# Gate/up of a hybrid encoder layer: where the part stores are issued, and how the next group's operands are split

## The chip, the cores and the metric

One core of one Trainium2 chip runs the whole kernel. The metric is the device time of one execution in microseconds (us); the median of three runs before the change is 2669.16 us. The engines are named as in the profile: PE (TensorE), PEld (its weight loads), DVE (VectorE), ACT (ScalarE), POOL (GpSimd), and SP (SyncE, which here only issues DMAs). ACT issues DMAs too, from the same in-order queue as its arithmetic.

## The reference

One layer of a streaming encoder is computed for 17 tiles of 128 tokens: 2048 prompt tokens and 8 streams of 16. A mixer (gated delta rule and a short convolution) and an output projection come first. What matters here is the last part, the feed-forward network:

```python
h = rmsnorm(x, norm_ffn_pre)
f = (jax.nn.silu(h @ w_gate) * (h @ w_up)) @ w_down
x = x + rmsnorm(f, norm_ffn_post)
```

with a model width of 1024 and a hidden width of 2816, all in float32.

## The kernel before

**Number format.** Each float32 operand v is split into a high part h, v rounded to the matmul's format by a cast on ACT, and a low part l = v - h, a subtraction on DVE or POOL. A product is three matmuls, hh, hl and lh. For the tokens' operands this split is made in `ffn_prep` (cast L893, subtraction L894), for the weights in `gu_weights` (cast L938, subtraction L939).

**Gate/up.** The tokens form three groups `FGROUPS` of 6, 6 and 5 tiles; the hidden width forms 22 columns f of 128 (`NF`). For each group the kernel walks over all 22 columns; one column of one group is called a block, (group, f). Gate and up are treated together as a 2x2 block product with the Strassen-Winograd scheme, so that a block takes 7 products instead of 8. A product has 12 matmuls (4 slices of the model width, 3 matmuls each, L963), a block 84, each with half a group's tokens as moving data: 384 columns for groups 0 and 1, 320 for group 2.

The 7 token operands of a group are named in `PARTS`: B11, T3, T1, T2, B21, T4, B22. Each consists of 4 slices (k), each a high tile xh and a low tile xl. T3 and a first sum are made by `ffn_sums`, T2 and T4 by one subtraction per slice inside `ffn_prep` (L887, L889), in place on the loaded half-tiles, so that one has to follow the other. The xh and xl tiles exist once: the split for the next group may be written only when PE has read the old group's tile for the last time.

**One block.** `gu_start` makes the first four products (B11, T3, T1, T2) into four PSUM banks b1, b3, b4, b2. `gate_up` then copies b1, b3 and b4 out by ACT (L999, L1000, L1001), and the other three products (B21, T4, B22) are added into those banks; each may begin only after the copy of its bank. Then come the recombination and the gating: u2 (DVE L1007), two additions on POOL (L1008, L1013), a SiLU (ACT L1010), c21 and c12 (DVE L1012, L1014), a second SiLU (ACT L1015), and the two gated results v1, v2 (DVE L1027, L1028). While this runs, `gu_start` of the next block goes ahead into four other banks.

Even and odd columns are combined for the down projection: an even block keeps v1 and v2 in a11 and a21; an odd block writes its own into a tile `pt` with six planes and makes four sums of them (L1034 to L1037). `pt` has one buffer. An odd block then stores `pt` to DRAM (`partd`), one DMA for each pair of token tiles, three in groups 0 and 1 and two in group 2 (L1039); an even block stores a11 with one DMA (L1041). Group 2 also stores its unpaired tile into `lastd` (L1031). All of these are issued on ACT's queue at the end of `gate_up`.

**Weights.** In group 0 the weights of a column are loaded, combined into sA to sD (L929 to L932), split, and the split ones are partly written to DRAM (`fsplit`); groups 1 and 2 reload them, and split again only three of the seven, except for the first two columns (`NSP`), of which all seven are reloaded. `ffetch` in `gate_up` runs one block ahead. The tiles sA to sD are used by group 0 alone.

**Change of group.** During columns 4 to 11 of a group the next group's eight half-tiles h are loaded, at column 16 `ffn_sums` runs on them, and after the last column `ffn_prep` makes all seven operands: 28 casts on ACT, 28 subtractions (L894), for even k on POOL and for odd k on DVE, and the 8 differences L887 and L889 on DVE. For group 0 the same work is done during the output projection.

**What sets the order.** The program is written in this order, but `TileContext(schedule_with_timeline_sim=True)` lets a planner sort the instructions of each engine: it steps through its own estimate of time, and of the instructions whose inputs it deems ready the one written first is issued first. An instruction written later can thus run earlier if it is ready earlier. On the chip each engine keeps the planned order, whatever comes late. Waits for tiles, banks and DMAs are set by the framework.

Of the kernel before, what the change touches and what calls it, by code (L numbers as in the profile page):

```python
# [10 lines left out]
F32R = mybir.dt.float32r  # L11
# [6 lines left out]
P = 128  # L18
# [4 lines left out]
NF = DFF // P  # L23
# [20 lines left out]
FGROUPS = [list(range(0, 6)), list(range(6, 12)), list(range(12, 17))]  # L44
# [25 lines left out]
def kernel(  # L70
# [28 lines left out]
    nc = tc.nc  # L99
    V, A, G, T = nc.vector, nc.scalar, nc.gpsimd, nc.tensor  # L100
# [7 lines left out]
    partd = [[dram.tile([len(g) // 2, P, 7, len(c) // 2, P], F32, name=f"partd{gi}_{ch}") for ch, c in enumerate(FCHUNKS)]  # L108
             for gi, g in enumerate(FGROUPS)]
    lastd = [dram.tile([P, 2, len(c) // 2, P], F32, name=f"lastd{ch}") for ch, c in enumerate(FCHUNKS)]  # L110
# [742 lines left out]
    KH = KD // 2  # L853
    PARTS = ("B11", "T3", "T1", "T2", "B21", "T4", "B22")
    HW = max(len(g) for g in FGROUPS) * P // 2
    with ExitStack() as ph:
        fp = ph.enter_context(tc.tile_pool(name="fp", bufs=1, reuse_waits="tile"))
# [12 lines left out]
        def ffn_sums(gi, hs, fs):  # L870
            hw = len(FGROUPS[gi]) * P // 2
            t3 = []
            for k in range(KH):
                b11, b12, b21, b22 = blocks(gi, hs, k)
                t3.append(fs.tile([P, HW], F32, tag="t3", name="ft3", bufs=KH)[:, :hw])
                V.tensor_sub(t3[k], b22, b12)
                V.tensor_sub(b12, b12, b11)
            return t3

        def ffn_prep(gi, hs, t3):  # L880
            hw = len(FGROUPS[gi]) * P // 2
            X = {nm: ([], []) for nm in PARTS}
            for nm in PARTS:
                for k in range(KH):
                    b11, b12, b21, b22 = blocks(gi, hs, k)
                    if nm == "T2":
                        V.tensor_sub(b12, b22, b12)  # L887
                    elif nm == "T4":
                        V.tensor_sub(b12, b21, b12)  # L889
                    v = {"B11": b11, "B21": b21, "B22": b22, "T3": t3[k]}.get(nm, b12)  # L890
                    h = fp.tile([P, HW], F32R, tag=f"xh{nm}{k}", name="xh")
                    l = fp.tile([P, HW], F32R, tag=f"xl{nm}{k}", name="xl")
                    A.copy(h[:, :hw], v)  # L893
                    (V if k % 2 else G).tensor_tensor(  # L894
                        out=l[:, :hw], in0=v, in1=h[:, :hw].bitcast(F32), op=ALU.subtract)
                    X[nm][0].append(h)
                    X[nm][1].append(l)
            return X

        with tc.tile_pool(name="fs", bufs=1, reuse_waits="tile") as fs:  # L900
            hs = list(ffn_load(0, fs))
            hid = ffn_prep(0, hs, ffn_sums(0, hs, fs))
        fe = ph.enter_context(tc.tile_pool(name="fe", bufs=1, reuse_waits="tile"))

        nw, early, wl = [0], [], []
# [50 lines left out]
        def product(ps, w, b, first):  # L956
            wh, wl = w
            bh, bl = b
            hw = ps.shape[-1]
            for k in range(KH):  # L960
                c = slice(k * P, (k + 1) * P)
                for ci, (w_, b_) in enumerate(((wh, bh), (wh, bl), (wl, bh))):
                    T.matmul(ps, w_[:, c], b_[k][:, :hw], start=(first and k == 0 and ci == 0),  # L963
                             stop=(k == KH - 1 and ci == 2), skip_group_check=not first)

        def gu_start(gi, f, X):
            hw = len(FGROUPS[gi]) * P // 2
# [17 lines left out]
        fd = side.enter_context(tc.tile_pool(name="fd", bufs=1, reuse_waits="tile", side="right"))  # L985
        ffetch(5 - NWE)

        def gate_up(gi, f, X, banks):
            n = len(FGROUPS[gi])
            hw = n * P // 2  # L990
            g_, f_, W, _ = fpend.pop(0)

            def ct(nm):
                return fb.tile([P, HW], F32, tag=nm, name=nm)[:, :hw]

            w = dict(zip(("A12", "A22", "S4"), W[4:]))
            b1, b3, b4, b2 = banks
            s1, s7, s5 = ct("m1"), ct("m7"), ct("m5")
            A.copy(s1, b1)  # L999
            A.copy(s7, b3)  # L1000
            A.copy(s5, b4)  # L1001
            product(b1, w["A12"], X["B21"], False)
            product(b3, w["A22"], X["T4"], False)
            product(b4, w["S4"], X["B22"], False)
            ffetch()
            u2 = ct("u2")
            V.tensor_add(u2, s1, b2)  # L1007
            G.tensor_tensor(out=s7, in0=s7, in1=s5, op=ALU.add)  # L1008
            sg0 = ct("m5")
            A.activation(sg0, b1, AF.Silu)  # L1010
            c21, c12 = ct("c21"), ct("c12")
            V.tensor_add(c21, u2, b3)  # L1012
            G.tensor_tensor(out=s7, in0=s7, in1=u2, op=ALU.add)  # L1013
            V.tensor_add(c12, u2, b4)  # L1014
            A.activation(c12, c12, AF.Silu)  # L1015
            ch, kk = FCH[f]
            q, c = kk // 2, len(FCHUNKS[ch]) // 2
            if kk % 2 == 0:
                a11 = fb.tile([P, HW], F32, tag="a11", name="a11", bufs=2)
                a21 = fb.tile([P, HW], F32, tag="a21", name="a21", bufs=2)  # L1020
                held[gi] = a11, a21
                v1, v2 = a11[:, :hw], a21[:, :hw]
            else:
                a11, a21 = held[gi]
                pt = fb.tile([P, 6, HW], F32, tag="pt", name="pt")
                v1, v2 = pt[:, 3, :hw], pt[:, 4, :hw]
            V.tensor_mul(v1, c21, sg0)  # L1027
            V.tensor_mul(v2, s7, c12)  # L1028
            if n % 2:
                for vi, v in enumerate((v1, v2)):  # L1030
                    nc.scalar.dma_start(out=lastd[ch][:, kk % 2, q, vi * 64:vi * 64 + 64], in_=v[:, hw - 64:hw])  # L1031
            if kk % 2:
                a11, a21, a12, a22 = a11[:, :hw], a21[:, :hw], v1, v2
                V.tensor_add(pt[:, 0, :hw], a21, a22)  # L1034
                V.tensor_sub(pt[:, 1, :hw], a11, a21)
                V.tensor_sub(pt[:, 2, :hw], pt[:, 0, :hw], a11)
                V.tensor_sub(pt[:, 5, :hw], pt[:, 2, :hw], a12)  # L1037
                for j in range(n // 2):
                    nc.scalar.dma_start(out=partd[gi][ch][j, :, 1:7, q, :], in_=pt[:, :, j * P:(j + 1) * P])  # L1039
            else:  # L1040
                nc.scalar.dma_start(out=partd[gi][ch][:, :, 0, q, :].rearrange("j p c -> p j c"),  # L1041
                                    in_=v1[:, :n // 2 * P].rearrange("p (j c) -> p j c", c=P))

        held, first_parts = {}, []
        for gi in range(len(FGROUPS)):
            if gi:
                hid = ffn_prep(gi, hs, t3)
            if gi + 1 < len(FGROUPS):
                hload, hs = ffn_load(gi + 1, fd), []
            for f in range(NF):  # L1050
                gate_up(gi, f, hid, started or gu_start(gi, f, hid))
                started = None
                if gi + 1 < len(FGROUPS):
                    if 4 <= f < 4 + KD:
                        with tc.issue_after(wl[0].ins):
                            hs.append(next(hload))
                    if f == NF - 6:
                        t3 = ffn_sums(gi + 1, hs, fd)
                elif f == 10:
                    side.close()  # L1060
                    dr = late.enter_context(tc.tile_pool(name="dr", bufs=1, reuse_waits="tile", side="right"))
                    c = len(FCHUNKS[0]) // 2
                    a = dr.tile([P, 2, c * P], F32, name="ar0")
                    nc.sync.dma_start(out=a, in_=partd[0][0][0, :, 0:2].rearrange("p i q c -> p i (q c)"))
                    first_parts = [dr.tile([P, 2, c * P], F32R, name=f"as0{i}") for i in range(2)]
                    for i, b in enumerate(first_parts):
                        A.copy(b[:, 0], a[:, i])
                        V.tensor_sub(b[:, 1], a[:, i], b[:, 0].bitcast(F32))
                    dprep += [down_chunk(ch) for ch in dorder]
                    prep_step(2)  # L1070
                elif 10 < f <= 10 + NDR:
                    prep_step(1)
# [203 lines left out]
```

## Time and profile before

| what | value |
|---|---|
| three runs | 2666.46, 2669.16, 2670.29 us |
| profiled execution, first to last instruction (its span) | 2659.7 us |
| the median of the runs less this span | 9.5 us |
| mean granted clock of PE | 0.978 |
| gate/up: first to last matmul of L963 | 1225.0 to 2167 us |
| DVE busy in gate/up (1225 to 2167.5) | 518.9 us |
| ACT, POOL busy there | 323.0, 473.7 us |
| DMA share there | 0.80 |

The span is that of one profiled execution; what lies around it in a run's time, the start and the end of a launch, is not in the profile, which gives no other time of that execution. In the profile's rows a line number is that of the kernel file; `xl<-fh,xh` names the tile written and the tiles read. An idle time in brackets is that of the engine just before the instruction, and the name behind the arrow is what ended it. "ACTq" is ACT's queue issuing a DMA, "issue" is time for which the profile shows no wait. The window view lists, for each stretch, its length, the engine's busy time and the instructions that touch it, the granted clock, the DMA share and the GB/s.

### The profile page before, as it was taken

The page shows a single profiled execution, that of the slowest core. Times are in us where ns is not written, and L with a number is a line of the kernel's source. Part 1 is how long each engine was busy: PE and PEld are TensorE (multiplying, and loading weights), DVE is VectorE, ACT ScalarE, POOL GpSimd, SP SyncE. Part 2 cuts the span into 40 slices and gives each one's busy share as a digit, 9 for nine tenths or more (in the row PEclk, how much of TensorE's full clock was granted, in tenths as well). Part 3 has the DMA queues.
Part 4 walks back from the last instruction along what each step waited for, and adds up shares of the span by engine and source line. Part 5 has one row for each costly group of instructions (what it writes and reads, how often), then busy time and mean ns, then how long its engine had stood idle before and what let it go on. Part 6 is the DMA issues. An engine that isn't in the chain of part 4 may idle for free.

```text
span 2659.7 us, 42363 instructions
## 1 busy us (share of the span) xinstructions
PE 2533.2 (95%) x15129; PEld 2357.1 (89%) x15129; DVE 1717.3 (65%) x3403; ACT 971.8 (37%) x2337; POOL 939.5 (35%) x841
## 2 busy tenths in 40 slices
PE   7989899999999989999999999999899999999997
PEld 6889789989899987878999999999899987887776
DVE  7788567667575875676978863433633344677698
ACT  5535115142251524433434432222323335333343
POOL 2321001000010210224556654443544445555563
PEclk9999989999999998999999999999999999999999
DMA  6876576666657555667877777877888852443365
GB/s 206 293 255 243 166 245 216 226 225 239 214 207 248 177 182 173 230 214 250 309 261 271 265 259 250 282 247 240 286 287 278 276 169 87 129 123 119 126 217 176
DMA packets 322403, 589.46 MB, mean 222 GB/s; under 512 B 57116, under 2 KB 206304, under 8 KB 303376
## 3 DMA queue, kind: packets, MB, share of 16 engines
q1 hardware_dynamic: 193600, 510.01, 56.7%
q10 hardware_dynamic: 128592, 76.74, 9.5%
q8 instruction: 120, 1.97, 0.3%
q14 instruction: 91, 0.75, 0.1%
HBM read 424.60 MB, written 162.05 MB: 221 GB/s over the span
## 4 chain that ended last, share of the span: by engine, by line
PE 67%; DVE 13%; DMA 8%; issue 4%; ACT 3%; POOL 2%; SPq 1%; ACTq 1%; DVEq 0%; POOLq 0%
PE fbank L963 28%; PE dbank L136 16%; PE fbank L1122 10%; PE tbank L758 3%; PE dbank L758 3%; DMA w<-wsplit 2%; DMA wr<-in_w_in 1%; DVE acc L367 1%; DVE xl L894 1%; POOL dw L829 1%; DMA dr<-in_w_dn 1%; DVE xr L1137 1%; DVE acc L1081 1%; DVE acc L1136 1%; DMA xt<-in_x 1%
## 5 line engine op out<-in xcount | busy, mean ns | idle before, releaser
L963 PE MATMUL fbank<-xh,fw 128*128 128x384 f32 (+1 forms) x3696 | 904.2, 327 | 19.7 <-ACT m L999 12.1
L136 PE MATMUL dbank<-hi,w 128*128 128x384 f32 (+1 forms) x2688 | 691.9, 336 | 16.6 <-DMA w<-wsplit 9.7
L963 PEld LDWEIGHTS fbank<-xh,fw 128*128 128x128 f32 x3696 | 654.9, 189 | 23.4 <-ACT m L999 14.2
L963 PE MATMUL fbank<-xl,fw 128*128 128x384 f32 (+1 forms) x1848 | 604.2, 327 | 0.0
L136 PEld LDWEIGHTS dbank<-hi,w 128*128 128x128 f32 x2688 | 484.8, 193 | 22.8 <-POOL w L340 8.4
L1122 PE MATMUL fbank<-dw,as 128*128 128x512 f32 x1980 | 463.2, 395 | 14.3 <-ACT dw L827 5.0
L1122 PEld LDWEIGHTS fbank<-dw,as 128*128 128x128 f32 x1980 | 372.0, 189 | 105.2 <-DVE acc L1081 7.4
L136 PE MATMUL dbank<-lo,w 128*128 128x384 f32 (+1 forms) x1344 | 449.5, 335 | 0.0
L963 PEld LDWEIGHTS fbank<-xl,fw 128*128 128x128 f32 x1848 | 348.9, 189 | 0.0
L136 PEld LDWEIGHTS dbank<-lo,w 128*128 128x128 f32 x1344 | 259.0, 193 | 1.7 <-issue 0.8
L1106 POOL TENSOR_TENSOR as<-ar,as 128x256 fp32r<-128x256 f32 (+1 forms) x207 | 188.2, 918 | 171.8 <-ACT as L1103 170.4
L939 POOL TENSOR_TENSOR fw<-rg,fw 128x512 fp32r<-128x512 f32 x124 | 176.5, 1424 | 180.9 <-ACT fw L938 180.7
L1081 DVE TENSOR_TENSOR acc<-acc,fbank 128x512 f32<-128x512 f32 x248 | 166.6, 682 | 99.6 <-PE fbank L1122 79.6
L1103 ACT CAST as<-ar 128x256 fp32r<-128x256 f32 (+1 forms) x288 | 118.3, 427 | 181.8 <-PE fbank L1122 132.7
L340 POOL TENSOR_TENSOR w<-wr,w 128x512 fp32r<-128x512 f32 x49 | 78.3, 1599 | 223.6 <-ACT w L338 188.0
L938 ACT CAST fw<-rg 128x512 fp32r<-128x512 f32 x124 | 77.5, 625 | 185.1 <-PE fbank L963 147.9
L367 DVE SCALAR_TENSOR_TENSOR acc<-R,cw,acc 128x384 f32<-128x384 f32 (+1 forms) x216 | 131.0, 609 | 2.0
L1007 DVE TENSOR_TENSOR u<-m,fbank 128x384 f32<-128x384 f32 (+1 forms) x66 | 34.8, 528 | 143.3 <-PE fbank L963 130.4
L1008 POOL TENSOR_TENSOR m<-m,m 128x384 f32<-128x384 f32 (+1 forms) x66 | 69.4, 1051 | 159.5 <-ACT m L1001 119.0
L939 POOL TENSOR_TENSOR fw<-ru,fw 128x512 fp32r<-128x512 f32 x62 | 92.3, 1488 | 85.8 <-ACT fw L938 70.2
L1012 DVE TENSOR_TENSOR c<-u,fbank 128x384 f32<-128x384 f32 (+1 forms) x66 | 34.9, 528 | 127.8 <-PE fbank L963 127.6
L552 POOL MEMSET AU<- 32x128 f32 x16 | 3.2, 197 | 281.0 <-PE gbank L538 272.1
(322 smaller groups left out, 3807.2 us busy)
## 6 DMA issues: line engine op xcount, KB each, us to landing
w<-wsplit SPq DMA_DIRECT2D x119, 1024.0 KB, 6.0
fw<-fsplit SPq DMA_DIRECT2D x188, 512.0 KB, 4.7
fsplit<-fw SPq DMA_DIRECT2D x94, 512.0 KB, 4.1
partd<-pt ACTq DMA_DIRECT2D x88, 384.0 KB, 6.0
rg<-in_w_gu SPq DMA_DIRECT2D x62, 512.0 KB, 3.7
wsplit<-w SPq DMA_DIRECT2D x28, 1024.0 KB, 4.7
wr<-in_w_in SPq DMA_DIRECT2D x98, 256.0 KB, 4.4
ar<-partd SPq DMA_DIRECT2D x48, 384.0 KB, 3.3
```

The costliest lines, as they stand in the source:

```text
L136: T.matmul(ps, l, r, start=(i == 0), stop=(i == n - 1))
L340: e.tensor_tensor(out=wl[:, c], in0=wr, in1=wh[:, c].bitcast(F32), op=ALU.subtract)
L367: V.scalar_tensor_tensor(acc, raw(d), w[:, d:d + 1], acc, op0=ALU.mult, op1=ALU.add)
L758: T.matmul(pss[n], m_[:, j, :], w_[k][:, n * 512:(n + 1) * 512], start=(k == 0 and ci == 0), stop=(k == KD - 1 and ci == 2))
L938: A.copy(w[:, 0], v)
L939: e.tensor_tensor(out=w[:, 1], in0=v, in1=w[:, 0].bitcast(F32), op=ALU.subtract)
L963: T.matmul(ps, w_[:, c], b_[k][:, :hw], start=(first and k == 0 and ci == 0), stop=(k == KH - 1 and ci == 2), skip_group_check=not first)
L1008: G.tensor_tensor(out=s7, in0=s7, in1=s5, op=ALU.add)
L1081: V.tensor_add(dst, dst, ps)
L1103: ins = A.copy(a[:, 0, :n], v)
L1106: e.tensor_tensor(out=a[:, 1, :n], in0=v, in1=a[:, 0, :n].bitcast(F32), op=ALU.subtract)
L1122: T.matmul(ps, a[:, x_, q * P:(q + 1) * P], w[:, y_], start=(start and q == 0 and ci == 0), stop=(q == c - 1 and ci == 2), skip_group_chec ...
```

## The change

Two things are done.

The part stores (L1031, L1039, L1041) are no longer issued where they are written: their arguments are put in a list `queued`, and the next block's `gate_up` issues them, in the program's order, right after its three bank copies. The last block of the last group issues its own at once.

The next group's operands are made in steps: `ffn_prep` now takes the dictionary X to fill and the names to make. B11 is made after column 20 of the old group. For group 1 it goes to tiles of its own, the high parts into four new tiles of the pool `fd`, the low parts into sA to sD; for group 2 it goes into the old B11 tiles, which are free since the end of group 0. T3, T1 and T2 are made after the last column, as before. B21, T4 and B22 are made inside the first block of the new group, behind its bank copies and the queued stores. For groups 1 and 2 all subtractions L894 are on DVE; for group 0 DVE and POOL trade even and odd k.

```diff
-        def ffn_prep(gi, hs, t3):
+        def ffn_prep(gi, hs, t3, X, names):
             hw = len(FGROUPS[gi]) * P // 2
-            X = {nm: ([], []) for nm in PARTS}
-            for nm in PARTS:
+            for nm in names:
+                X[nm] = ([], [])
                 for k in range(KH):
...
-                    h = fp.tile([P, HW], F32R, tag=f"xh{nm}{k}", name="xh")
-                    l = fp.tile([P, HW], F32R, tag=f"xl{nm}{k}", name="xl")
+                    if gi == 1 and nm == "B11":
+                        h = fd.tile([P, HW], F32R, tag="xh", name="xh", bufs=KH)
+                        l = fe.tile([P, 512], F32R, tag="s" + "ABCD"[k], name="xl")
+                    else:
+                        h = fp.tile([P, HW], F32R, tag=f"xh{nm}{k}", name="xh")
+                        l = fp.tile([P, HW], F32R, tag=f"xl{nm}{k}", name="xl")
                     A.copy(h[:, :hw], v)
-                    (V if k % 2 else G).tensor_tensor(
+                    (G if not gi and k % 2 else V).tensor_tensor(
                         out=l[:, :hw], in0=v, in1=h[:, :hw].bitcast(F32), op=ALU.subtract)
...
+        FIRST, REST = PARTS[:4], PARTS[4:]
...
-            hid = ffn_prep(0, hs, ffn_sums(0, hs, fs))
+            hid = ffn_prep(0, hs, ffn_sums(0, hs, fs), {}, PARTS)
...
             A.copy(s5, b4)
+            for q in queued:
+                nc.scalar.dma_start(**q)
+            queued.clear()
+            if "B21" not in X:
+                ffn_prep(gi, hold["hs"], hold["t3"], X, REST)
             product(b1, w["A12"], X["B21"], False)
...
-                    nc.scalar.dma_start(out=partd[gi][ch][j, :, 1:7, q, :], in_=pt[:, :, j * P:(j + 1) * P])
+                    queued.append(dict(out=partd[gi][ch][j, :, 1:7, q, :], in_=pt[:, :, j * P:(j + 1) * P]))
...
+            if (gi, f) == (len(FGROUPS) - 1, NF - 1):
+                for q in queued:
+                    nc.scalar.dma_start(**q)
...
             if gi:
-                hid = ffn_prep(gi, hs, t3)
+                hid = ffn_prep(gi, hs, t3, hold["X"], FIRST[1:])
+                hold.update(hs=hs, t3=t3)
...
                     if f == NF - 6:
                         t3 = ffn_sums(gi + 1, hs, fd)
+                    elif f == NF - 2:
+                        hold["X"] = ffn_prep(gi + 1, hs, t3, {}, FIRST[:1])
```

The stores of L1031 and L1041 are queued in the same way.

More of the change, by code (lines that the diff above doesn't have):

```diff
@@ L1030, in gate_up @@
                 for vi, v in enumerate((v1, v2)):
-                    nc.scalar.dma_start(out=lastd[ch][:, kk % 2, q, vi * 64:vi * 64 + 64], in_=v[:, hw - 64:hw])
+                    queued.append(dict(out=lastd[ch][:, kk % 2, q, vi * 64:vi * 64 + 64], in_=v[:, hw - 64:hw]))
             if kk % 2:
@@ L1038, in gate_up @@
                 for j in range(n // 2):
-                    nc.scalar.dma_start(out=partd[gi][ch][j, :, 1:7, q, :], in_=pt[:, :, j * P:(j + 1) * P])
+                    queued.append(dict(out=partd[gi][ch][j, :, 1:7, q, :], in_=pt[:, :, j * P:(j + 1) * P]))
             else:
-                nc.scalar.dma_start(out=partd[gi][ch][:, :, 0, q, :].rearrange("j p c -> p j c"),
-                                    in_=v1[:, :n // 2 * P].rearrange("p (j c) -> p j c", c=P))
-        held, first_parts = {}, []
+                queued.append(dict(out=partd[gi][ch][:, :, 0, q, :].rearrange("j p c -> p j c"),
+                                   in_=v1[:, :n // 2 * P].rearrange("p (j c) -> p j c", c=P)))
+            if (gi, f) == (len(FGROUPS) - 1, NF - 1):
+                for q in queued:
+                    nc.scalar.dma_start(**q)
+        held, first_parts, queued, hold = {}, [], [], {}
         for gi in range(len(FGROUPS)):
             if gi:
-                hid = ffn_prep(gi, hs, t3)
+                hid = ffn_prep(gi, hs, t3, hold["X"], FIRST[1:])
+                hold.update(hs=hs, t3=t3)
             if gi + 1 < len(FGROUPS):
```

## The prediction

> **What bounds the kernel now.** I read the page first: 2659.7 us of span, TensorE (PE) busy for 95% of it. So only stretches where PE is not fed count. The change touches gate/up alone, so I cut that stage by PE's matmuls of L963 in windows at the blocks' first matmuls (a block is one column f of one group: 84 matmuls, 22 blocks to a group). The columns are stretch, length, PE busy (instructions touching it), granted clock, DMA share, GB/s.
>
> ```profile
> span 2659.7 us, 42363 instructions
> PE 2533.2 (95%) x15129; PEld 2357.1 (89%) x15129; DVE 1717.3 (65%) x3403; ACT 971.8 (37%) x2337; POOL 939.5 (35%) x841
> ...
> 1225.04:1247.08 22.04, 16.76 (x84) 0.92 0.56 185
> 1247.08:1400.17 153.09, 147.82 (x842) 1.00 0.86 300
> 1400.17:1560.33 160.16, 160.16 (x926) 1.00 0.79 276
> 1560.33:1581.22 20.89, 17.19 (x85) 0.84 0.61 187
> 1581.22:1886.98 305.76, 305.76 (x1766) 1.00 0.80 259
> 1886.98:1908.37 21.39, 14.19 (x86) 0.93 0.94 315
> 1908.37:2167.00 258.63, 258.63 (x1764) 1.00 0.80 258
> ```
>
> The fifth stretch holds 21 blocks of group 1 with PE never idle: 305.76 / 21 = 14.56 us a block, PE's own pace. The last gives group 2, with narrower tiles, 258.63 / 21 = 12.32. Against these, four stretches lose time: block (0,0) 22.04 - 14.56 = 7.48; blocks (0,1) to (0,10) 153.09 - 145.60 = 7.49; the first block of group 1 20.89 - 14.56 = 6.33; the first of group 2 21.39 - 12.32 = 9.07. Blocks (0,11) to (0,21) are 11 x 14.56 = 160.16 to the last digit. So the stage holds 30.4 us of loss; the change can touch the last three, **22.9 us**. That is the ceiling.
>
> PE's timeline and its waits say what ends each loss; the last row is PE's weight loads waiting for L1001 within 1240 to 1410 us.
>
> ```profile
> 1572.52 0.69 PE L963 MATMUL fbank<-xh,fw 128*128 128x384 f32 x1 [3.70 <-ACT m L999]
> ...
> 1896.52 0.41 PE L963 MATMUL fbank<-xh,fw 128*128 128x320 f32 x1 [2.35 <-ACT m L999]
> 1905.15 0.48 PE L963 MATMUL fbank<-xh,fw 128*128 128x320 f32 x1 [4.85 <-ACT m L1001]
> ...
> PEld fbank L963 <- ACT m L1001: 4.0, 4, 2.0
> ```
>
> Always it is a copy out of a bank by ScalarE (ACT): the second half of a block may not add into a bank before its copy is out. At the start of group 1 the idle 3.70 costs 6.33 because the clock drops (0.84 in that row). Why was the copy late? ACT's timeline, a window of DVE, and the groups of DVE and of POOL from 1548.43 to 1571.0:
>
> ```profile
> 1571.57 0.52 ACT L1015 ACTIVATE c<-c 128x384 f32<-128x384 f32 x1 [1.22 <-DVE c L1014]
> 1572.00 0.46 ACT L999 COPY m<-fbank 128x384 f32<-128x384 f32 x1
> ...
> 1548.43:1572.00 23.57, 23.54 (x27) 0.98 0.79 269
> ...
> L894 DVE TENSOR_TENSOR xl<-fh,xh 128x384 fp32r<-128x384 f32 x10 | 11.9, 1202 | 0.0
> L889 DVE TENSOR_TENSOR fh<-fh 128x384 f32<-128x384 f32 x4 | 4.4, 1118 | 0.0
> L894 DVE TENSOR_TENSOR xl<-ft,xh 128x384 fp32r<-128x384 f32 x2 | 2.7, 1367 | 0.0
> L887 DVE TENSOR_TENSOR fh<-fh 128x384 f32<-128x384 f32 x4 | 2.5, 642 | 0.0
> ...
> L894 POOL TENSOR_TENSOR xl<-fh,xh 128x384 fp32r<-128x384 f32 x11 | 13.6, 1261 | 3.8 <-ACT xh L893 3.8
> ```
>
> L999 stands behind the SiLU L1015, that behind VectorE's (DVE) L1014, and DVE has been busy 23.54 of 23.57 us with the next group's operands: up to L1014 (its 0.5 us end where L1015 starts, so it began near 1571.0), 12 splits (L894) and 8 differences, 21.5 us together, while POOL makes the other splits. The price of one depends on the neighbour, as the timelines of both show:
>
> ```profile
> 1556.29 1.03 DVE L887 TENSOR_TENSOR fh<-fh 128x384 f32<-128x384 f32 x2
> 1557.23 0.55 DVE L894 TENSOR_TENSOR xl<-fh,xh 128x384 fp32r<-128x384 f32 x1
> 1563.35 3.95 DVE L894 TENSOR_TENSOR xl<-fh,xh 128x384 fp32r<-128x384 f32 x3
> ...
> 1554.52 1.32 POOL L1008 TENSOR_TENSOR m<-m,m 128x384 f32<-128x384 f32 x1
> 1557.94 3.77 POOL L894 TENSOR_TENSOR xl<-fh,xh 128x384 fp32r<-128x384 f32 x3 [2.10 <-ACT xh L893]
> 1561.67 1.33 POOL L1013 TENSOR_TENSOR m<-m,u 128x384 f32<-128x384 f32 x1
> 1562.97 3.91 POOL L894 TENSOR_TENSOR xl<-fh,xh 128x384 fp32r<-128x384 f32 x3
> ```
>
> POOL is idle from 1555.84 to 1557.94: there DVE gets through two operations in 0.94 us (1556.29 to the next start, 1557.23), 0.47 each. Beside three POOL splits, three of DVE take 3.95: 1.3 each. That factor is the heart of the sum.
>
> **The change part by part. First, the operands.** Nothing is saved in count: 28 casts, 28 splits and 8 differences per group stay, all 28 splits now on DVE. Four (B11) go ahead of the last block; their room is DVE's idle before this row, after the old spare tiles' last reader:
>
> ```profile
> 1540.04 0.69 DVE L939 TENSOR_TENSOR fw<-sD,fw 128x512 fp32r<-128x512 f32 x1 [3.17 <-ACT fw L938]
> ...
> 1543.88 0.56 DVE L1012 TENSOR_TENSOR c<-u,fbank 128x384 f32<-128x384 f32 x1 [2.69 <-PE fbank L963]
> ```
>
> 4 x 0.47 = 1.9 of 2.69 us: hidden (without that cover, 1.9). POOL keeps its two additions per block (L1008, L1013), each holding one DVE operation at 1.3 instead of 0.47: 1.7 us. Suppose, against the change, that all 24 other splits still come before L1014: from 1548.43, 32 x 0.47 = 15.0, three block operations (L1035, L1007, L1012) x 0.47 = 1.4, plus 1.7, gives 1566.5; L1014 0.5, L1015 0.5, L999 0.5: **1568.0**. PE's second half of that block is due at 1560.33 + 48/84 x 14.56 = **1568.65**. So the L999 wait goes, by 0.6 us at worst; with B22's four behind L1014 by 2.5. What is late next is L1001, due 4.16 later at 1572.8. Of the new waits: the casts of B21, T4 and B22 stand on ACT behind the first block's three copies, and the product of B21 waits for them and for four DVE splits; by the same count all 24 are done by about 1568, so none is late.
>
> Group 2 by its own rows:
>
> ```profile
> 1874.89 1.17 DVE L894 TENSOR_TENSOR xl<-fh,xh 128x320 fp32r<-128x320 f32 x1
> 1882.66 0.48 DVE L894 TENSOR_TENSOR xl<-fh,xh 128x320 fp32r<-128x320 f32 x1
> 1883.06 1.56 DVE L887 TENSOR_TENSOR fh<-fh 128x320 f32<-128x320 f32 x2
> ...
> 1863.24 2.17 ACTq L1039 DMA_DIRECT2D partd<-pt  x3
> ...
> 1898.63 5.95 ACTq L1039 DMA_DIRECT2D partd<-pt  x3
> 1904.67 0.43 ACT L1001 COPY m<-fbank 128x320 f32<-128x320 f32 x1 [7.06 <-issue]
> ```
>
> The step is 0.40 (1882.66 to 1883.06): 1874.89 + 32 x 0.40 + 1.4 + 1.7 = 1890.8, L999 by 1892.3, due at 1886.98 + 7.04 = 1894.0. The 2.35 wait goes too.
>
> **Second, the part stores.** Each odd block issues three from ACT. Their order is the planner's (it sorts each engine by its own estimate of readiness):
>
> ```profile
> 1299.14 0.63 ACT L938 CAST fw<-sD 128x512 fp32r<-128x512 f32 x1
> 1302.51 1.99 ACTq L1039 DMA_DIRECT2D partd<-pt  x3
> 1304.60 0.48 ACT L1001 COPY m<-fbank 128x384 f32<-128x384 f32 x1 [4.83 <-DVE sD L932]
> ```
>
> L938 is written in the program after the same block's L1001 and runs before it; the stores, written before L999 of this block, run after it. So emitting the stores three copies later only lowers their rank: where the planner finds `pt` ready before the bank, they stay. I take them as **unmoved** in group 0, worth 0; the ends are 0 and 7.5, with 4.0 (the waits for L1001 above) if only those vanish. In the first block of group 2 the stores took 5.95 us before L1001. With L1015 done near 1891.9, four operations of `pt` put the issue at 1894 to 1895.5; at the 2.17 of the nearest group-1 row L1001 ends by 1898.1, due at 1886.98 + 7.04 + 3.52 = 1897.5; at 5.95, 1901.9. So 0 to 4.4 remains; I take 1.0, near the 2.17. For group 1 the same count (issue 1570 to 1572) leaves 0 to 1.8; I take 0.5. Later stores also free `pt` later, but DVE has room:
>
> ```profile
> 1581.22:1857.86 276.64, 100.62 (x140) 1.00 0.80 255
> ```
>
> Group 0's own operands only trade odd and even between DVE and POOL, 14 each: 0, at most one operation (1.3) either way, under the output projection. Later stages are unchanged and start earlier.
>
> **Sum.** 6.33 - 0.5 + 9.07 - 1.0 = 13.9 us off the profiled execution: a span of 2645.8. The median of the runs, 2669.16, is 9.5 above this span; I carry that, so 2655.3.
>
> **The rivals.** *The stores do move behind the copies*: the sum without residuals is 15.4, and group 0 gives 4.0 to 7.49, so 19.4 to 22.9: 2646.3 to 2649.8. Against it stands the planner's order above. *VectorE stays the bound*, so slower: the dear price is then not POOL's doing. With 24 splits at 1.2 (1202 ns above) and eight differences at 0.87 (6.9 / 8), L1014 comes at 1548.43 + 28.8 + 7.0 + 1.4 = 1585.6, not 1571.0: 14.6 us worse, and times 12.32 / 14.56 another 12.4 at group 2: 2696. It decides where the mean price passes (1571.0 - 1548.43 - 1.4) / 32 = 0.66 us. Against it speak the 0.47 steps while POOL idles. The Trainium skill (Perfetto Trace Analysis, Optimizing Scalar/DVE Operations) has a rule on this side: when VectorE is saturated, handing some of its work to GpSimd may make sense, though it doubts that between these two, since they share a read port. VectorE is saturated here (23.54 of 23.57), so by that rule the change goes the wrong way, to this rival's time; by the rows 14 more splits at 0.47 are 6.6 us more, and 14 splits and 8 differences no longer made dear save more than that (21.5 - 20 x 0.47 = 12.1). *Half works*: the planner, seeing more DVE work, puts splits before L1012 or `pt`, or the third store queues again; 4 to 11 of the 15.4 us stay: 2658 to 2665. *It does nothing on balance*: the wait for L999 becomes one for splits or stores of like size, 2664 to 2673.
>
> **How the numbers follow.** Chances: forecast, 2652 to 2658, 0.43; stores move 0.17; half works 0.20; nothing 0.11; slower 0.09. What a measurement can tell is 0.2%, 5.3 us, so from 2663.8 to 2674.5 is the same. Faster: 0.43 + 0.17 + 0.16 of "half" = 0.76; same 0.04 + 0.11 = 0.15; slower 0.09. The range from 2646 to 2668 leaves out the slower rival and about half of "nothing".
>
> **What would show it.** Right: blocks (1,0) and (2,0) within 1.5 us of 14.56 and 12.32; POOL without L894 in gate/up; L894 on DVE near 0.5 us; stretch (0,1) to (0,10) still near 153; stores between L1000 and L1001 there. Wrong: L894 on DVE above 0.66; PE waiting for L894 in (1,0); the stores after L1001 in group 0 with 146 us for that stretch.

## The result, and the profile after

The changed kernel's median is 2656.42 us (2653.60 to 2658.92, 4 runs), that of the kernel before 2669.72 (2666.46 to 2672.27, 4 runs): a ratio of 0.9953, 95% interval 0.9937 to 0.997. The change was measured twice more, each time beside the kernel before on one chip: 0.9968 (0.9954 to 0.9983) and 0.9955 (0.9938 to 0.9973). So it is faster by 0.3 to 0.5%. The prediction's 2655.3 and its range hold the time, the closeness in part by luck (below). Its sum does not hold in every term, and the profile says which.

The same cut of gate/up as in the prediction, at the first matmuls of the blocks, in the changed kernel's profile, whose span is 2651.8 us (the matmuls are line L969 there; the columns are stretch, length, PE busy, granted clock, DMA share, GB/s):

```profile
1226.71:1249.86 23.15, 17.88 (x84) 0.85 0.58 197
1249.86:1400.07 150.21, 147.26 (x841) 1.00 0.87 302
1400.07:1560.23 160.16, 160.16 (x925) 1.00 0.80 273
1560.23:1575.56 15.33, 15.07 (x85) 1.00 0.71 232
1575.56:1881.88 306.32, 306.32 (x1766) 1.00 0.83 261
1881.88:1894.19 12.31, 12.31 (x85) 1.00 0.90 306
1894.19:1913.39 19.20, 15.18 (x86) 0.82 0.95 321
1913.39:2159.96 246.57, 246.57 (x1682) 1.00 0.82 258
```

Read against 14.56 and 12.32 us a block: the first block of group 1 loses 0.77 instead of 6.33, and the first of group 2 nothing instead of 9.07. But the second block of group 2, (2,1), which lost 0.2 before, now loses 19.20 - 12.32 = 6.88. Blocks (0,1) to (0,10) lose 4.61 instead of 7.49. Block (0,0) loses 8.59 here instead of 7.48, but 7.5 in both repeats, so that is not the change. And 21 blocks of group 1 in which PE is never idle take 306.32 us instead of 305.76.

The new loss has a plain chain on ScalarE's (ACT's) timeline:

```profile
1887.99 0.43 ACT L1007 COPY m<-fbank 128x320 f32<-128x320 f32 x1 [0.82 <-DVE pt L1038]
...
1892.78 5.94 ACTq L1009 DMA_DIRECT2D partd<-pt  x3
1898.82 0.44 ACT L1021 ACTIVATE m<-fbank 128x320 f32<-128x320 f32 x1 [6.83 <-PE fbank L969]
...
1901.31 0.47 ACT L1026 ACTIVATE c<-c 128x320 f32<-128x320 f32 x1 [0.50 <-issue]
...
1902.94 0.62 ACT L827 CAST dw<-dr 128x512 fp32r<-128x512 f32 x1 [1.17 <-DVE dr L815]
1903.47 0.42 ACT L1005 COPY m<-fbank 128x320 f32<-128x320 f32 x1
...
1906.75 0.62 ACT L827 CAST dw<-dr 128x512 fp32r<-128x512 f32 x1 [2.35 <-DVE dr L815]
1907.28 0.42 ACT L1006 COPY m<-fbank 128x320 f32<-128x320 f32 x1
```

PE waits for the two copies:

```profile
1903.94 0.41 PE L969 MATMUL fbank<-xh,fw 128*128 128x320 f32 x1 [2.55 <-ACT m L1005]
1907.75 0.64 PE L969 MATMUL fbank<-xh,fw 128*128 128x320 f32 x1 [1.48 <-ACT m L1006]
```

The three stores take 5.94 us to issue, as they did before (5.95). They no longer stand before the bank copy (now L1007), which is done by 1888.42; they stand before the first SiLU (now L1021). The gating of block (2,0) is late by that, its second SiLU (L1026) too, and behind that come the copies of block (2,1). Directly before each of the two late copies stands a cast (L827) of the early loads for the down projection, the prefetch, which had waited for a difference on DVE (L815); earlier casts of L827, at 1899.15, had stood behind the stores too. L1005 was due at 1894.19 + 7.04 = 1901.23 and ran at 1903.47. The two waits make 4.03 of the 6.88 us; the rest are matmuls made longer by the lower clock (0.82 in that row, 15.18 us busy instead of 12.31).

### The profile page after: what moved, and what is told of

Its sections match the earlier page's. It is cut to its first block, busy times and chain, and to the rows that moved or that the text cites. A ratio compares the mean times of both kernels' runs of the same rounds, so it can differ in the third digit from the quotient of the medians.

```text
span 2651.8 us, 42346 instructions
## 1 busy us (share of the span) xinstructions
PE 2533.6 (96%) x15129; PEld 2357.8 (89%) x15129; DVE 1710.2 (64%) x3431; ACT 972.9 (37%) x2337; POOL 915.1 (35%) x813
## 4 chain that ended last, share of the span: by engine, by line
PE 43%; DVE 7%; issue 3%; POOL 2%; DMA 2%; ACT 1%; ACTq 1%; POOLq 0%; DVEq 0%; SPq 0%
PE fbank L969 30%; PE fbank L1139 10%; PE tbank L758 1%; PE dbank L758 1%; DVE xl L898 1%; POOL dw L829 1%; DMA dr<-in_w_dn 1%; DVE acc L1098 1%; DVE xr L1154 1%; DVE acc L1153 1%; POOL as L1123 1%; DMA fh<-hTd 0%; ACTq L1009 0%; DMA mr<-mixd 0%; PE ftbank L781 0%
## 5 line engine op out<-in xcount | busy, mean ns | idle before, releaser
L969 PE MATMUL fbank<-xh,fw 128*128 128x384 f32 (+1 forms) x3696 | 904.1, 327 | 10.8 <-ACT m L1005 6.9
L136 PE MATMUL dbank<-hi,w 128*128 128x384 f32 (+1 forms) x2688 | 691.7, 336 | 18.0 <-DMA w<-wsplit 10.4
L969 PEld LDWEIGHTS fbank<-xh,fw 128*128 128x128 f32 x3696 | 654.0, 189 | 14.1 <-ACT m L1005 8.6
L969 PE MATMUL fbank<-xl,fw 128*128 128x384 f32 (+1 forms) x1848 | 604.2, 327 | 0.0
L969 PEld LDWEIGHTS fbank<-xl,fw 128*128 128x128 f32 x1848 | 348.8, 189 | 0.0
L1019 POOL TENSOR_TENSOR m<-m,m 128x384 f32<-128x384 f32 (+1 forms) x66 | 70.5, 1068 | 150.4 <-ACT m L1007 97.6
```

The costliest lines, as they stand in the source:

```text
L136: T.matmul(ps, l, r, start=(i == 0), stop=(i == n - 1))
```

## The experiments

All kernels are compared by their own profiles, cut in the same way: "loss" is a stretch less 14.56 or 12.32 us per block. "Gate/up" runs from the first matmul to the end of the last. Ratios are to the kernel before on the same chip, with the 95% interval.

| kernel | (0,1)-(0,10) | (1,0) | (1,1)-(1,21) | (2,0) | (2,1) | gate/up | ratio |
|---|---|---|---|---|---|---|---|
| before | 7.49 | 6.33 | 0.00 | 9.07 | 0.19 | 942.4 | |
| before again | 8.63 | 5.54 | 0.00 | 8.82 | 0.00 | 942.3 | |
| changed | 4.61 | 0.77 | 0.56 | 0.00 | 6.88 | 933.2 | 0.9953 (0.9937-0.997) |
| changed, second | 6.17 | 0.03 | 0.56 | 0.00 | 6.70 | 932.8 | 0.9968 (0.9954-0.9983) |
| changed, third | 6.54 | 0.03 | 0.56 | 0.00 | 4.63 | 931.1 | 0.9955 (0.9938-0.9973) |
| operands only | 6.94 | 0.03 | 2.11 | 0.00 | 4.84 | 933.5 | 0.9969 (0.9955-0.9983) |
| stores only | 6.47 | 6.83 | 0.00 | 2.92 | 7.44 | 943.0 | 1.0003 (0.9989-1.0018) |
| POOL shares | 4.35 | 3.82 | 0.56 | 3.55 | 7.25 | 938.8 | 1.0000 (0.9988-1.0012) |
| VectorE only | 6.83 | 0.00 | 0.00 | 0.00 | 4.21 | 930.3 | 0.9970 (0.9958-0.9982) |
| late prefetch | 5.55 | 0.77 | 0.56 | 0.00 | 0.00 | 926.7 | 0.9937 (0.9921-0.9954) |
| three stores on SP | 4.51 | 0.03 | 0.56 | 0.00 | 0.47 | 925.9 | 0.9954 (0.9940-0.9969) |
| VectorE only, SP | 8.65 | 0.00 | 1.68 | 0.00 | 4.91 | 934.6 | 0.9958 (0.9944-0.9972) |
| the same, stores behind | 4.26 | 1.03 | 0.00 | 0.68 | 0.47 | 927.0 | 0.9942 (0.9925-0.9960) |
| VectorE only, prefetch moved | 8.33 | 0.00 | 0.00 | 0.00 | 0.00 | 927.6 | 0.9945 (0.9923-0.9967) |

The ratios are wide because the time ahead of gate/up varies: its first matmul starts between 1224.8 and 1233.6 us in these profiles, whatever the kernel. Gate/up itself repeats to 0.1 us before and to some 2 us changed. So the verdicts below rest on the table's stretches, and the ratios say only whether the time agrees.

**One half at a time.** Operands only: the changed kernel, the queue emptied where the stores were written before.

```diff
-            for q in queued:              # behind A.copy(s5, b4)
-                nc.scalar.dma_start(**q)
-            queued.clear()
...
-            if (gi, f) == (len(FGROUPS) - 1, NF - 1):
-                for q in queued:
-                    nc.scalar.dma_start(**q)
+            for q in queued:
+                nc.scalar.dma_start(**q)
+            queued.clear()
```

> The operands in steps and on VectorE, the part stores issued where they were. Theory (the operands carry the gain): the first block of group 1 falls from 20.9 us to 15 to 16, L894's successor on VectorE is near 0.5 us, and the kernel is 6 to 12 us faster than before (2658 to 2664); blocks 1 to 10 of group 0 keep about 7.5 us of loss, and at the start of group 2 the three stores again stand in front of L1001, so 3 to 5 us stay there. Rival (the stores carry it): first block of group 1 near 20, no more than 3 us faster. Second rival (the two are worth little apart, the store order is what lets the operands pay): (2,0) and (2,1) together lose as much as before, 9 us, and the gain is 5 us.

Stores only: the kernel before, with the queue.

```diff
+            for q in queued:              # behind A.copy(s5, b4)
+                nc.scalar.dma_start(**q)
+            queued.clear()
...
-                    nc.scalar.dma_start(out=partd[gi][ch][j, :, 1:7, q, :], in_=pt[:, :, j * P:(j + 1) * P])
+                    queued.append(dict(out=partd[gi][ch][j, :, 1:7, q, :], in_=pt[:, :, j * P:(j + 1) * P]))
```

> The part stores queued behind the next block's copies, the operands as before. Theory (operands carry the gain): first block of group 1 stays at 20 to 21 us; the stretch (0,1) to (0,10) loses 4 to 5 us instead of 7.5; at the start of group 2 the wait for L1001 may go (up to 5 us); in all 2 to 6 us faster, 2663 to 2668. Rival (the planner leaves the stores where they were): no difference, within 1 us, same order of issue on ScalarE. Rival (stores carry it): 10 us or more faster.

The operands carry the gain: 0.9969 against 0.9968 for the whole change on the same chip. The stores alone are worth nothing, 1.0003; the 2 to 6 us that the theory expected of them did not come. Their rows for the first two blocks of group 2, and those of "operands only":

```profile
1888.68:1903.92 15.24, 12.84 (x86) 1.00 0.88 292
1903.92:1923.67 19.75, 14.96 (x86) 0.83 0.78 262
```

```profile
1889.38:1901.69 12.31, 12.31 (x86) 1.00 0.89 306
1901.69:1918.85 17.16, 14.36 (x87) 0.90 0.96 328
```

Stores alone: 2.92 + 7.44 = 10.4 us of loss against 9.3 before. The third store, 4.86 us of issue, went behind L1001 there; the wait left L1001 and came back one block later. Operands only: a loss of 4.84 in (2,1) as well, and here ACT issues its three stores behind the bank copy although they are written ahead of it (1899.99, the copy at 1895.21):

```profile
1895.21 0.43 ACT L1007 COPY m<-fbank 128x320 f32<-128x320 f32 x1 [0.82 <-DVE pt L1035]
...
1899.99 6.20 ACTq L1052 DMA_DIRECT2D partd<-pt  x3
1906.30 0.44 ACT L1018 ACTIVATE m<-fbank 128x320 f32<-128x320 f32 x1 [6.67 <-PE fbank L969]
```

So at this place the operands' edit moved the stores. Probably the planner, seeing more work on VectorE (DVE), deems `pt` ready later and sets the copy first; its estimates are not in the profile. Here the queue was not needed for that, and neither order spares the 6 us of issue.

**Both kernels once more.** No edit.

> The changed kernel once more, for its second profile. Theory (a new stall in the second block of group 2, made by the three stores of the last block of group 1 that hold ScalarE's queue for 5.9 us in front of the SiLU L1021): the block (2,1) is again 17 to 20 us instead of 12.3, the third store's issue again 3 to 5 us, ratio 0.995. Rival (a chance collision of this one profile): (2,1) within 1 us of 12.3, third issue near 1.3 us.

> The kernel before once more, for a second profile. If the profiled execution of before was simply a quick one, this one's span lies 3 to 9 us higher (2663 to 2669), with the difference in the stages ahead of gate/up or behind it, and gate/up again loses 30 us with 6.3 at (1,0) and 9.1 at (2,0). If gate/up itself varies, its losses in blocks 1 to 10 of group 0 differ by several us from 7.5.

> The changed kernel beside these two on the same chip, for the comparison alone: gate/up 932 to 934 us, (2,1) losing 6 to 7 us, ratio to before 0.995 to 0.997.

The stall in (2,1) is no chance: 6.88, 6.70 and 4.63 us. The kernel before repeats too, 942.4 and 942.3 us of gate/up; its second span is 2667.3 against 2659.7, and 6.1 of these 7.6 us lie ahead of gate/up (first matmul at 1231.1 against 1225.0). The profiled execution that the prediction worked from was a quick one.

**Which part of the operands' edit pays?** POOL shares: the changed kernel, half of the splits of groups 1 and 2 on POOL again.

```diff
-                    (G if not gi and k % 2 else V).tensor_tensor(
+                    (G if (k % 2 if not gi else k % 2 == 0) else V).tensor_tensor(
```

> The changed kernel with the splits of groups 1 and 2 shared again by VectorE and POOL, half each; steps and stores as changed. Theory (the price of a VectorE operation beside POOL, 1.3 us instead of 0.47, made the wait): the splits on VectorE cost about 1.0 us in the mean again, the loss in the first block of group 1 comes back, 4 to 6 us instead of 0 to 0.8, and gate/up takes 937 to 942 us instead of 933. Rival (the steps made the gain: B11 early, the rest late): (1,0) keeps a loss below 1.5 us, gate/up within 1.5 us of 933.

VectorE only: the kernel before, with the engine of the splits as its only edit.

```diff
-                    (V if k % 2 else G).tensor_tensor(
+                    (V if k % 2 or gi else G).tensor_tensor(
```

> The kernel before with nothing changed but the engine: all splits of groups 1 and 2 on VectorE, in one step after the last column, stores as before. Theory (the engine alone does it): (1,0) loses less than 2 us, gate/up 933 to 936 us. Rival (the steps are needed): VectorE's 28 splits in one piece reach L1014 late and (1,0) loses 3 to 6 us, gate/up 938 to 942.

VectorE only, first block of group 1, blocks (1,1) to (1,21), and the first two of group 2:

```profile
1567.44:1582.00 14.56, 14.56 (x85) 1.00 0.74 222
1582.00:1887.76 305.76, 305.76 (x1765) 1.00 0.83 261
1887.76:1900.08 12.32, 12.32 (x86) 1.00 0.91 314
1900.08:1916.61 16.53, 14.19 (x87) 0.90 0.98 336
```

One word in one line does all of it: nothing is lost at (1,0) and (2,0), with the operands in one step and the stores as before. With the steps but POOL sharing, 3.82 and 3.55 us come back and the ratio is 1.0000. The loss at (1,0) fell just short of the 4 to 6 that theory had set; the steps are worth 2 us or so there, but only while POOL shares. Once VectorE works alone they bring nothing to these blocks.

The same edit also changes the planner's order: the first copy no longer stands behind the SiLU L1015. That order is a rival to the price. In "POOL shares" the copy of (1,0) runs ahead of the SiLU too, and still ends at 1569.24, 1.6 us after it is due (1559.34 + 8.32 = 1567.66), so the order alone does not do it. In "VectorE only" L1015 starts 3.97 us after the first matmul of (1,0), against 11.24 before, and 5.39 us after that of (2,0), against 8.65. The planner put 7 and 4 splits behind L1014 there. Had they come first, at 0.47 and 0.40 us each, and the copy after the SiLU as before, it would end some 8.3 and 7.9 us after that matmul, by estimate; due are 8.32 and 7.04. So the price takes away the wait of group 1 and all but some 0.9 us of the 2.35 of group 2; the new order does the rest.

**What makes the stall in (2,1)?** At the change to group 2 the planner also starts the prefetch for the down projection (a load of parts and four loads of 512 KB of weights, casts on ACT, differences on DVE), though it is written at column 10. In the changed kernel the four are issued just before the stores of 1892.78, the last at 1890.51:

```profile
1888.71 1.28 SPq L808 DMA_DIRECT2D dr<-in_w_dn  x3
```

At the change to group 1, where no prefetch runs, the same three stores stand before the same SiLU, take 2.37 us, and (1,1) loses 0.03. Late prefetch: those loads held until column 10.

```diff
-                    nc.sync.dma_start(out=a, in_=partd[0][0][0, :, 0:2].rearrange("p i q c -> p i (q c)"))
+                    with tc.issue_after(wl[0].ins):
+                        nc.sync.dma_start(out=a, in_=partd[0][0][0, :, 0:2].rearrange("p i q c -> p i (q c)"))
...
-                    prep_step(2)
+                    with tc.issue_after(wl[0].ins):
+                        prep_step(2)
```

(and likewise for the four later steps)

> The changed kernel, with the loads for the down projection (first parts and first weights) held until the column where the program writes them, instead of where the planner puts them, the first blocks of group 2. Theory A (ScalarE's queue is held by the three stores themselves): the third store still takes over 3 us and (2,1) still loses 5 to 7 us. Theory B (the prefetch makes the stall: its 2 MB of loads hold up the stores, and its casts and differences stand between the block's own): the third store takes 1 to 1.5 us, (2,1) loses less than 1 us, gate/up takes 926 to 927 us instead of 933, and the kernel is 6 us faster than the changed one if the down projection does not start later for it (491.8 us from the end of gate/up).

Three stores on SP: the prefetch stays, the stores leave ACT.

```diff
-                nc.scalar.dma_start(**q)
+                (nc.sync if (gi, f) == (2, 0) else nc.scalar).dma_start(**q)
```

> The changed kernel, with the three stores of the last block of group 1 issued from SP instead of ScalarE; the prefetch for the down projection stays. Theory A (the stores on ScalarE's queue make the stall): (2,1) loses less than 1.5 us, gate/up 927 to 928 us. Theory B (the prefetch's casts and differences make it): L1021 is no longer late, but the copies L1005 and L1006 of (2,1) are, behind the casts L827 that wait for VectorE's differences, and (2,1) keeps 2 to 5 us.

Late prefetch, ACT at the same place and the block (2,1); then the stores on SP:

```profile
1899.44 2.25 ACTq L1009 DMA_DIRECT2D partd<-pt  x3
1901.79 0.44 ACT L1021 ACTIVATE m<-fbank 128x320 f32<-128x320 f32 x1 [5.65 <-PE fbank L969]
```

```profile
1901.45:1913.77 12.32, 12.32 (x86) 1.00 1.04 334
```

```profile
1896.84 3.46 SPq L1009 DMA_DIRECT2D partd<-pt  x3
```

```profile
1898.23:1911.02 12.79, 12.58 (x86) 1.00 1.06 370
```

Without the prefetch the three issues take 2.25 us and no time is lost. With the prefetch but the stores on SP, 0.47 is lost. So in the changed kernel either cure suffices: theory B for why the issue is slow, theory A for whom it hurts. "Late prefetch" takes the slow issue and the casts away together, so it does not part the two. The stretch behind gate/up took 497.2 us in it instead of 491.5 to 494.8; its profiled execution was the slowest of its four runs (2659.37, median 2651.30), and one profile does not say whether the late loads did that.

**The smallest edits together.** VectorE only, and the three stores written for SP:

```diff
-                    nc.scalar.dma_start(out=partd[gi][ch][j, :, 1:7, q, :], in_=pt[:, :, j * P:(j + 1) * P])
+                    (nc.sync if (gi, f) == (1, NF - 1) else nc.scalar).dma_start(
+                        out=partd[gi][ch][j, :, 1:7, q, :], in_=pt[:, :, j * P:(j + 1) * P])
```

> The kernel before with two edits only: all splits of groups 1 and 2 on VectorE (one step, stores where they were), and the three stores of the last block of group 1 issued from SP. Theory (what the change gains comes from VectorE having the splits alone; what it leaves comes from the third store held up on ScalarE's queue): (1,0), (2,0) and (2,1) together lose less than 1.5 us, the B11 steps of groups 1 at the old pace (0.0 instead of 0.6), gate/up 925 to 927 us, 14 to 17 us faster than before in gate/up; time near 0.994 of before if the down projection keeps 492 to 495. Rival (the steps are needed once the stall is gone): (2,1) keeps 3 us or more, gate/up 929 or more.

This missed: (2,1) loses 4.91 us still, 1.68 more went in one block of group 1 (a wait for a copy in (1,10), where "operands only" lost 1.55; not explained), and gate/up takes 934.6. These are the rival's numbers, but the last run below, also without the steps, loses nothing, so it is not the steps that are missing. ACT and DVE in (2,1):

```profile
1906.73 0.34 ACTq L1031 DMA_DIRECT2D lastd<-a  x1
1907.17 0.42 ACT L1000 COPY m<-fbank 128x320 f32<-128x320 f32 x1 [2.99 <-DVE a L1028]
```

```profile
1902.85 0.68 DVE L815 TENSOR_TENSOR dr<-dr 128x512 f32<-128x512 f32 x1
1903.45 1.78 DVE L819 TENSOR_TENSOR dr<-dr 128x512 f32<-128x512 f32 x1
1905.15 1.54 DVE L1028 TENSOR_TENSOR a<-m,c 128x320 f32<-128x320 f32 x1
```

L1000 stands on ACT behind a small store (L1031) of a result that DVE makes in L1028, and on DVE the prefetch's differences L815 and L819 come first. The stores on ACT are one way for the prefetch to do harm, its work on DVE another: theory B's second half. In "three stores on SP" the same copy came at 1906.93, due at 1898.23 + 7.04 + 1.76 = 1907.03; here it was due 1895.56 + 8.80 = 1904.36. PE was 2.7 us further on, the prefetch was not.

Next, all part stores forced behind the third copy (VectorE only, the queue, SP for the three):

```diff
-            A.copy(s5, b4)
+            c4 = A.copy(s5, b4)
+            with tc.issue_after(c4.ins):
+                for q in queued:
+                    (nc.sync if (gi, f) == (2, 0) else nc.scalar).dma_start(**q)
+            queued.clear()
```

> The same, and every part store forced behind the next block's third bank copy on ScalarE. Theory (in group 0 the stores in front of L1001 make the even blocks' part of the loss): the even blocks 4, 6, 8 and 10 of group 0 lose less than 0.5 us together instead of 3 to 5; the stretch (0,1) to (0,10) falls to 2 to 4 us, gate/up 922 to 924. Rival (the loss there is VectorE's, late for the SiLU, and the stores only stand in the gap): the stretch stays at 4 to 8 us, or the loss moves to the odd blocks, gate/up 925 to 930.

The even blocks 4, 6, 8 and 10 of group 0 lose 0.0 together, where the kernel before lost 0.7, 0.2, 1.0 and 2.9 and the run beside it 0.8, 0.4, 1.4 and 3.2. Blocks 3, 5, 7 and 9 keep 1.7, 0.3, 0.9 and 1.3, 1.3 to 1.5 us more together than in those two, and (0,11), without loss before, loses 1.27. So the stores in front of the copy do cost what the even blocks lose, as the theory has it, but about half of it comes back in the odd ones: the stretch, 4.26, and gate/up, 927.0, lie in the rival's ranges. Blocks (1,0) and (2,0) lose 1.03 and 0.68 as well, which they did not in "VectorE only".

Last, VectorE only with the prefetch written at column 3 and held behind that column's weight load, so that it misses the change of group:

```diff
-                elif f == 10:
+                elif f == 3:
...
-                    prep_step(2)
+                    with tc.issue_after(wl[0].ins):
+                        prep_step(2)
...
-                elif 10 < f <= 10 + NDR:
-                    prep_step(1)
+                elif 3 < f <= 3 + NDR:
+                    with tc.issue_after(wl[0].ins):
+                        prep_step(1)
```

(the first load is held in the same way)

> The kernel before with two edits only: all splits of groups 1 and 2 on VectorE, and the loads for the down projection written at column 3 of group 2 and held behind that column's weight load, so that they miss the change of group. Theory (two causes, VectorE beside POOL and the prefetch beside the change of group): third store 1 to 1.5 us, (1,0), (2,0) and (2,1) together lose less than 1.5 us, a loss of at most 2 us at columns 4 to 7 of group 2 instead, gate/up 925 to 928 us, down projection 492 to 495, and 0.993 to 0.995 of before. Rival (the prefetch's work on VectorE costs the same wherever it stands): columns 4 to 7 lose 4 to 7 us together, gate/up 930 or more.

```profile
1897.35 2.38 ACTq L1039 DMA_DIRECT2D partd<-pt  x3
```

```profile
1565.33:1579.89 14.56, 14.56 (x86) 1.00 0.71 224
1579.89:1885.65 305.76, 305.76 (x1766) 1.00 0.82 261
1885.65:1897.96 12.31, 12.31 (x86) 1.00 0.75 247
1897.96:1910.28 12.32, 12.32 (x87) 1.00 0.99 301
1910.28:2156.84 246.56, 246.56 (x1682) 1.00 0.84 271
```

Every block of groups 1 and 2 runs at PE's pace, columns 4 to 7 included. Gate/up takes 927.6 us, 3.5 to 5.6 less than in the changed kernel although its group 0 was a dear one (8.33), and what follows takes 491.5. Its median is 2653.56 us, ratio 0.9945 (0.9923 to 0.9967). The times alone do not set it apart from the changed kernel; the stretches do.

## Why the prediction was right, and where it was not

**The ceiling and the two prices: right.** PE lost time only where the sum said, in both profiles of before. On the changed kernel a split on DVE takes some 544 ns at 384 columns and 474 to 483 at 320. Beside POOL it can take up to 1368 (POOL's splits in group 0) and 1299 (its addition L1019 in group 2). POOL makes no split after 1150.0, when group 0's are done:

```profile
L898 DVE TENSOR_TENSOR xl<-fh,xh x60: 474/544/1368, 1116.7 to 1888.2; 128x384 fp32r<-128x384 f32 x36, 128x320 fp32r<-128x320 f32 x24
L898 POOL TENSOR_TENSOR xl<-fh,xh x12: 997/1266/1433, 1118.3 to 1150.0; 128x384 fp32r<-128x384 f32 x12
```

The price can fall on POOL instead. The sum let each of POOL's additions hold one DVE operation at 1.3 us; at the change to group 2 the addition L1024 took 5.16 us, against 1.02 in the median of its 66, while the splits of 320 columns beside it kept 474 to 476 ns (spans on POOL are rough, but it is not the splits that became dear):

```profile
1879.42 5.16 POOL L1024 TENSOR_TENSOR m<-m,u 128x384 f32<-128x384 f32 x1 [3.77 <-DVE u L1018]
```

"POOL shares" and "VectorE only" turn the same loss on and off by the engine alone, the planner's order having a small part in group 2 (above). The Trainium skill (SBUF — State Buffer, Who interferes with whom) says that a VectorE operation with two SBUF inputs and a GpSimd one that reads SBUF contend for a shared port; the trace agrees, 544 ns against up to 1368 at 384 columns. What the Trainium skill (Perfetto Trace Analysis, Optimizing Scalar/DVE Operations) offers on the other side, to relieve a saturated VectorE by GpSimd, did not hold for this pair, as that section itself doubts: taking 14 splits back onto a DVE that was busy 23.54 of 23.57 us shortened its work at group 1, from 21.6 us for 22 operations to 18.7 for 36 in "VectorE only".

**Group 1: right in size.** Predicted 0.5 us left in (1,0), measured 0.77, 0.03 and 0.03. The copy was counted ready at 1568.0 against 1568.65. It came earlier and by another way:

```profile
1566.68 0.47 ACT L1005 COPY m<-fbank 128x384 f32<-128x384 f32 x1
1568.13 0.53 ACT L1026 ACTIVATE c<-c 128x384 f32<-128x384 f32 x1 [0.97 <-DVE c L1025]
```

The planner set the copy ahead of the SiLU that the sum had in front of it. By the sum's own order the copy would have followed L1026 and ended near 1569.1, half a us late. The size is right partly by luck: the 0.5 was taken for stores in front of the third copy, but they came last (1575.19), and PE waited 0.26 us for the copy L1007 alone.

**Group 2: the step that failed.** "At 5.95, 1901.9. So 0 to 4.4 remains; I take 1.0" followed the stores only as far as L1001. The price stayed, 5.94 us; L1001 was set ahead of them; and I named nobody who waits behind L1001. It was the SiLU of the same block, and through it and the prefetch's casts the copies of the next: 6.88, 6.70 and 4.63 us in (2,1) instead of 1.0. I also chose 2.17, the price of a block without the prefetch, for a place that has it; the runs without it there show 2.25 and 2.38. Of the rivals, "half works" had this clause, "the third store queues again", with 4 to 11 us staying. At the two changes of group 7.65, 6.73 and 4.66 us stayed: by its mechanism that was the case that came about.

**Group 0: "unmoved, worth 0" was half right.** In the changed kernel's blocks (0,4) and (0,6) one of the three stores does go behind the copy:

```profile
1304.28 0.96 ACTq L1009 DMA_DIRECT2D partd<-pt  x2
1305.34 0.48 ACT L1007 COPY m<-fbank 128x384 f32<-128x384 f32 x1 [3.39 <-DVE sB L937]
1305.37 0.86 ACTq L1009 DMA_DIRECT2D partd<-pt  x1
```

In (0,8) and (0,10) none does. Over the profiles above, the stretch (0,1) to (0,10) loses 5.5 us in the mean where the stores are queued without force (7 profiles, 4.35 to 6.54) and 7.8 where they are not (6, 6.83 to 8.65). That is some 2.3 us of gain, between the ends 0 and 4.0 of the prediction.

**The sum.** 13.9 us were predicted for the profiled execution. Gate/up gave 9.1, 9.5 and 11.2 against 942.3: more left in group 2, 2.3 more from group 0, 0.56 lost to a term that the sum lacked (below), and 1.1 more lost in (0,0) in the first of the three. That the median lies so near to 2655.3 is luck in part. The medians of the first comparison differ by 13.3 us, those of the two others by 7.8 and 11.1; the second's ratio, 0.9968, makes 2660.6 of 2669.16, outside the forecast's 2652 to 2658 and inside "half works". The scaling was wrong too: what lies around the span is 1.8 us (2653.60 less 2651.8 for one and the same execution of the changed kernel), not 9.5. The rest of the 9.5 was the difference between a quick execution and the median. It cancelled, since the gain was carried over as a difference.

## What to carry to other kernels

Before giving a second engine half of a job, look at the price of one operation while that engine is idle and while it works; here sharing made the whole slower than one engine alone. Where a blocking instruction is moved back in an in-order queue, follow it past the wait that it caused to whatever stands behind its new place, for that inherits the price. And where a planner sorts by readiness, the order in the text is a wish: read the order from the trace, or tie it to an instruction.

## What the runs showed of the hardware that was not expected

Three stores of 384 KB issued together from ACT held its queue for 4.67 to 6.87 us in the seven profiles that issue them together on ACT just behind the four loads of 512 KB, and for 2.25 and 2.38 us where these were moved away. The DMA share during the issue was 0.99 in the changed kernel, 0.87 and 0.72 in those two. So the issuing engine, not only the transfer, pays when other transfers are under way; what holds its queue was not tried.

In all seven profiles of kernels that keep group 1's B11 in the spare tiles PE loses 0.56 us over blocks (1,1) to (1,21) without ever being idle ("operands only" lost a further 1.55 there), and the kernels that keep B11 in its old place do not: 306.32 against 305.76 us, or 0.027 us a block. Within a block the matmuls of the product with that operand take 175.0 ns each in the mean and those of the next product 173.9; all others take 173.3, as all do without the spare tiles. Why was not tried.
